# Moving 62 transfers of a transformer kernel from SyncE's queue to GpSimd's

## The chip, the cores and the metric

The kernel runs on one core of a Trainium2 chip, as one program. The metric is device time in microseconds, from several executions: the median of three runs before the change is 4835.77 us (4834.83 to 4836.31). The engines are named as in the profile: PE (TensorE's matmuls; PEld its weight loads), DVE (VectorE), ACT (ScalarE), POOL (GpSimd) and SP (SyncE). SP computes nothing here. It issues transfers between the chip's main memory (DRAM) and the on-chip buffers; POOL and ACT can issue transfers too. An instruction that has to wait holds up all that stands behind it on the same engine.

## The reference

Two layers of a hybrid transformer block over 512 latent tokens and 256 context tokens of width 1024. Cut to what matters:

```python
for l in range(2):
    with_ctx = l < 1                            # layer 1 leaves out the context's branch results
    h_lat = rmsnorm(x_lat, norm1_g[l]) * (1 + sc1) + sh1          # the same for the context
    p = h_lat @ w_in[l]                         # ssm input, q, k, v of two attentions, three gates
    ys, yd, yn = ssm_mixer(...), diff_mixer(...), na_mixer(...)   # three branches
    m = sigmoid(g_ssm) * (ys @ w_br_ssm) + sigmoid(g_diff) * (yd @ w_br_diff) + sigmoid(g_na) * (yn @ w_br_na)
    x_lat = x_lat + g1 * (m @ w_out[l])
    h2 = rmsnorm(x_lat, norm2_g[l]) * (1 + sc2) + sh2
    x_lat = x_lat + g2 * peer_ffn(h2, ...)      # 8 heads x 16 of 16384 experts per token
    # in layer 0 the context tokens go the same way
return rmsnorm(x_lat, final_norm_g)
```

`peer_ffn` scores keys, takes the best 16 pairs for each head, and sums `gelu(u_i . h2) * g_i * v_i` over the chosen experts. All arithmetic is float32.

## The kernel before

Tokens are in six tiles of 128 (0 and 1 context, 2 to 5 latent). The state x, the branches' results, gates, q, k and v are kept in DRAM tensors between the stages: `xs` (one 512 KB entry for each tile), `ybuf` (branch results, eight chunks of 128 channels), `hn` (the next layer's normalised tiles) and others.

**A layer's stages.** `front` makes the normalised tokens `hh`, `hl`, projects, runs the state-space and attention branches, and then merges: `merge` loads the branch results (`yt`, eight loads, two buffers, each split at once into a high part `yh` and a rest `yl`), multiplies by `w_br`, gates, multiplies by `w_out`, adds to x, and stores each tile to `xs`. Layer 0 merges twice (context, latent), layer 1 once; beside layer 0's merges stand the matmuls of the next layer's modulation (`ada_w`). The expert stage follows. `prepared` and `normed` load pairs of tiles from `xs` into the one buffer `nx` of their pool, `root` squares them on ACT and takes the reciprocal root on DVE, `normed_tile` scales (`ny`), transposes on PE and modulates, and the result is split into `h2`. Two pools of this kind are at work in layer 0, one for the latent tiles and one for the context's. Then `early` multiplies all 128 blocks of `peer_u` by `h2` (PE tile `s`), beside the choice of experts (`chosen`, `route`), while tokens of a few tiles (0 and 1 in layer 0, 2 in layer 1) get their experts by gathers (`gathered`, tile `grow`, on POOL). `experts` multiplies 128 blocks of `peer_v` (PE tile `stay`); `finish` adds x to each tile's result and stores it to `xs` in layer 0 (to the output in layer 1); `renew` normalises the tile for layer 1 and stores it to `hn`, from which `front` of layer 1 loads it again.

**Precision.** Each float32 operand is split into two parts (`split`: a cast on ACT, L61, and a subtraction on DVE, L62), and three matmuls are done (L70 to L72). Weights are streamed: `chunk` loads 512 KB into a rotating buffer (`raw`; `row()` takes buffers of the same kind for rows of x) and splits it.

**Queues and order.** All plain transfers, except results of `early` and the gate tables (which ACT issues), go through one helper on SP, so in the profile they all have the line L58:

```python
    def dma(self, out, in_):
        self.nc.sync.dma_start(out, in_)
```

POOL issues only the gathers (L1206). The loops of a stage are woven by hand with costs (`weave`), and that gives each instruction its priority; the final order on each engine is written out when the program is built, by a scheduler that follows priorities and its own model of times. On the chip each engine then runs its list strictly in order, and waits where an operand or a buffer isn't ready. Buffers of a new stage lie where buffers of an old one lay, and wait for those to be read.

Of the kernel before, what the change touches and what calls it, by code (L numbers as in the profile page):

```python
# [50 lines left out]
class Net:  # L51
# [4 lines left out]

    def dma(self, out, in_):
        self.nc.sync.dma_start(out, in_)  # L58

    def split(self, x, hi, lo):  # L60
        self.nc.scalar.copy(hi, x)  # L61
        self.nc.vector.tensor_sub(lo, x, hi.bitcast(F32))  # L62
# [412 lines left out]
    def normed(self, src, r, scale, shift, p, pg):  # L475

        tmp = pg.tile([128, 8, 256], F32, name="ntmp", tag="gst")
        for i, ap in enumerate(src):
            x = p.tile([128, D], F32, name="nx", bufs=1)
            self.dma(x, ap)  # L480
            y = p.tile([128, D], F32, name="ny", bufs=1)
            self.normed_tile(x, y, tmp[:, :, 128 * i:128 * i + 128], r, scale, shift, p)
        return tmp
# [448 lines left out]
    def merge(self, l, x, t0, n, p):  # L932

        nc, v = self.nc, self.nc.vector
        ts = slice(t0, t0 + n)
        yh, yl, mh, ml = [p.tile([128, 8, n], F32R, name=a, bufs=1) for a in ("yh", "yl", "mh", "ml")]
        for k in range(8):
            t = p.tile([128, n], F32, name="yt")
            self.dma(t, self.ybuf[l][k, :, ts])
            self.split(t, yh[:, k], yl[:, k])  # L940
            yield 0.50
        for j in range(4):
            w = self.wchunk(self.a["w_br"][l, j])
            for h in range(2):
                c = slice(128 * h, 128 * h + 128)
                g = p.tile([128, 3, n], F32, name="g3")
                self.dma(g, self.gbuf[l][2 * j + h, :, :, ts])
                for b, (k0, nk) in enumerate(((0, 2), (2, 4), (6, 2))):
                    ps = self.ps1("mg")
                    self.mm3(ps[:, :n], lambda k: (w[0][:, k0 + k, c], w[1][:, k0 + k, c]),  # L950
                             lambda k: (yh[:, k0 + k], yl[:, k0 + k]), nk)
                    v.scalar_tensor_tensor(g[:, b], g[:, b], 1.0, ps[:, :n], op0=ALU.add, op1=ALU.mult)
                    if b:
                        v.tensor_add(g[:, 0], g[:, 0], g[:, b])
                self.split(g[:, 0], mh[:, 2 * j + h], ml[:, 2 * j + h])
            yield 5.00
        tiles = range(t0 // 128, (t0 + n) // 128)
        gate = {}
        for r in sorted({1 if i < 2 else 0 for i in tiles}):
            gate[r] = p.tile([128, D], F32, name=f"g1{r}", bufs=1)  # L960
            self.dma(gate[r], self.arow[l][r:r + 1, 2 * D:3 * D].to_broadcast([128, D]))
        xt = {}
        for i in tiles:
            xt[i] = p.tile([128, D], F32, name=f"x{i - tiles[0]}", bufs=1)
            self.dma(xt[i], x[i])
        for j in range(4):
            w = self.wchunk(self.a["w_out"][l, j])
            c = slice(256 * j, 256 * j + 256)
            for i in reversed(tiles):
                t = slice(128 * i - t0, 128 * i - t0 + 128)  # L970
                ps = self.ps1("mg")
                self.mm3(ps[:, :256], lambda k: (mh[:, k, t], ml[:, k, t]), lambda k: (w[0][:, k], w[1][:, k]), 8)
                d = p.tile([128, 256], F32, name="d")
                v.scalar_tensor_tensor(d, ps[:, :256], 0.5, gate[1 if i < 2 else 0][:, c], op0=ALU.mult, op1=ALU.mult)
                v.tensor_add(xt[i][:, c], xt[i][:, c], d)
            yield 4.00
        for i in reversed(tiles):
            self.dma(self.xs[i], xt[i])

    def part(self, t0, n, x):  # L980
        t = slice(t0, t0 + n)
# [320 lines left out]
    def finish(self, l, i, acc, to):  # L1302

        v, p = self.nc.vector, self.sp
        r = 0 if i > 1 else 1
        if r not in self.gate:
            self.gate[r] = self.row()
            self.dma(self.gate[r], self.arow[l][r:r + 1, 5 * D:6 * D].to_broadcast([128, D]))
        x = self.row()
        self.dma(x, self.xs[i])  # L1310
        v.tensor_mul(to, acc, self.gate[r])  # L1311
        v.tensor_add(to, to, x)  # L1312
        if l < DEPTH - 1:
            self.dma(self.xs[i], to)
        else:
            if "f" not in self.gate:
                self.gate["f"] = self.row()
                self.dma(self.gate["f"], self.a["final_g"].to_broadcast([128, D]))
            v.tensor_scalar_mul(x, to, self.root(to, x, p))  # L1319
            v.tensor_mul(x, x, self.gate["f"])  # L1320
            self.dma(self.out[i - 2], x)

    def renew(self, l, i, x):

        h = self.row().rearrange("p (k t) -> p k t", k=8)
        self.normed_tile(x, self.row(), h, 0 if i > 1 else 1, self.nscale[l + 1][0], self.acol[l + 1][:, 0:8], self.sp, wide=True)
        self.dma(self.hn[i], h)

    def hidden(self, ph):
        self.hh = ph.tile([128, 8, NT], F32R, name="hh")  # L1330
# [2 lines left out]
    def front(self, l):  # L1333

        x = self.a["x"] if l == 0 else self.xs
        kinds = range(l, 2)
        with ExitStack() as right, ExitStack() as left:
            self.hidden(right.enter_context(self.pool("h", side="right")))
            own = right.enter_context(ExitStack())
            if l == 0:  # L1340
                prep = self.ssm_prep(l, own.enter_context(self.pool("sprep", side="right")))
                with self.psum(mm=3, un=3, sm=2), self.pool("norm", 2) as p:
                    self.drain(self.weave((self.start(l, p), 40.0), (prep, 40.0), lead=True))
            else:
                prep = iter(())
                with self.pool("norm", 2, "right") as p:
                    for i in range(6):
                        t = p.tile([128, 8, 128], F32, name="hn")
                        self.dma(t, self.hn[i])
                        self.part(128 * i, 128, t)  # L1350

            def states():
                yield from prep
                own.close()
                with self.pool("ssm", 1, "right") as p:
                    yield from self.ssm(l, p)
                if l < DEPTH - 1:
                    with self.pool("sprep", 1, "right") as p:
                        yield from self.ssm_prep(l + 1, p)

            def mixers(p):
                def attends(u):
                    for g in kinds:
                        yield from self.attend(l, g, u, p)

                cost = 84.0 if l == 0 else 72.0
                yield from self.project(l, 0, p)
                yield from self.weave((self.project(l, 1, p), 48.0), (attends(0), cost))
                yield from self.weave((self.project(l, 2, p), 48.0), (attends(1), cost))
                yield from attends(2)  # L1370

            pg = left.enter_context(self.pool("gate"))
            with self.stream(3, 4), self.psum(sc=2, mm=3, sm=2, gt=1), self.pool("att") as p:
                self.att_consts(l, p)
                self.drain(self.weave((mixers(p), 500.0 if l == 0 else 450.0), (states(), 300.0 if l == 0 else 200.0),
                                      (self.gates(l, pg), 187.0 if l == 0 else 125.0)))
        with self.stream(3, 4), self.psum(mg=5, mm=3), self.pool("next", 2) as q:
            def merges():
                for g in kinds:
                    with self.pool("mg", 2) as p:  # L1380
                        yield from self.merge(l, x, LCTX * g, LLAT if g else LCTX, p)

            jobs = [(merges(), 70.0)]
            if l < DEPTH - 1:
                jobs.append((self.modulation(l + 1, range(24), q), 72.0))
            self.drain(self.weave(*jobs))
# [174 lines left out]
```

## Time and profile before

| what | value |
|---|---|
| median of three runs | 4835.77 us |
| profiled execution | 4839.11 us, its span 4837.2 us |
| mean granted TensorE clock | 0.956 |
| PE busy | 4437.8 us (92%) |
| DVE busy | 3786.0 us (78%) |
| ACT busy | 1849.3 us (38%) |
| POOL busy | 1130.1 us (23%) |
| bytes moved | 1215.18 MB, mean 251 GB/s |

The shares are of the whole span; a stage can have quite another limit. The page shows PE at 70 to 80% in a few of its 40 slices, at the passages between stages, and POOL at nothing outside the gathers' two stretches. SP's instructions are all issues of transfers: the time beside one is that of the issue, not of the transfer. A merged row (x4) spans from the first of its instructions to the end of the last.

### The profile page before, as it was taken

Reading aid. Unit: us, or ns where it says so; the run is one execution under the profiler, and the core shown is the slowest. Engines: PE = TensorE matmul, PEld = TensorE weight load, DVE = VectorE, ACT = ScalarE, POOL = GpSimd, SP = SyncE. Lnnn points to the kernel's source line nnn. Section 1 sums busy time; section 2 is a strip of 40 time slices with the busy share of each in tenths; the row PEclk is TensorE's granted clock in tenths of the full one; section 3 lists DMA queues with packets and bytes.
Section 4 is the critical chain, followed back from the end, with each engine's and each line's share of the span. In section 5 each row is a group of like instructions: output and inputs, shape, how many; then the busy total and the mean of one; then the engine's idle time right before and its main releaser. Section 6 shows DMA issues by size and latency. Waiting matters only on the chain. (4 is left out here: it accounts for less than half of the span.)

```text
span 4837.2 us, 68859 instructions
## 1 busy us (share of the span) xinstructions
PE 4437.8 (92%) x24197; PEld 3718.5 (77%) x24197; DVE 3786.0 (78%) x8760; ACT 1849.3 (38%) x3019; POOL 1130.1 (23%) x772
## 2 busy tenths in 40 slices
PE   8998998869988999879999998999879999989998
PEld 4787886668776777658888877887769899978887
DVE  8377985758988999987887764877555799968888
ACT  3244454434322345443222223445233355533333
POOL 0000000000465355533343300000000133324552
PEclk9999998979999999989999998999889999999999
DMA  7453435844898789999999945533444599989997
GB/s 244 153 146 99 144 118 178 271 149 134 301 334 306 253 317 335 360 351 377 361 339 351 344 173 176 147 118 97 169 133 144 174 338 351 344 325 379 371 374 269
DMA packets 462839, 1215.18 MB, mean 251 GB/s; under 512 B 47691, under 2 KB 181915, under 8 KB 458907
## 3 DMA queue, kind: packets, MB, share of 16 engines
q1 hardware_dynamic: 311002, 690.61, 41.9%
q0 software_dynamic: 110592, 402.70, 22.7%
q10 hardware_dynamic: 40896, 117.46, 6.2%
q8 instruction: 190, 3.11, 0.3%
q14 instruction: 159, 1.29, 0.1%
HBM read 1031.54 MB, written 179.04 MB: 250 GB/s over the span
## 5 line engine op out<-in xcount | busy, mean ns | idle before, releaser
L1206 POOL DMA_INDIRECT grow<-in_u_rows,pick x384 | 515.3, 1342 | 2944.3 <-DVE cand L1078 1201.7
L61 ACT CAST hi<-raw 128x1024 fp32r<-128x1024 f32 x490 | 513.2, 1051 | 893.0 <-PE s L71 590.5
L62 DVE TENSOR_TENSOR lo<-raw,hi 128x1024 fp32r<-128x1024 f32 x490 | 595.5, 1218 | 290.5 <-ACT hi L61 287.2
L72 PE MATMUL s<-h2h,lo 128*128 128x512 f32 (+1 forms) x2048 | 762.4, 373 | 54.6 <-DVE lo L62 54.2
L70 PE MATMUL s<-h2h,hi 128*128 128x512 f32 (+1 forms) x2048 | 772.2, 377 | 12.3 <-ACT eact L1244 9.2
L1206 POOL DMA_INDIRECT grow<-in_v_rows,pick x384 | 614.7, 1601 | 696.6 <-PE stay L1277 251.0
L71 PE MATMUL s<-h2l,hi 128*128 128x512 f32 (+1 forms) x2048 | 761.4, 372 | 0.2 <-DVE h2l L62 0.2
L1274 PE MATMUL stay<-hiv,wh 128*128 128x512 f32 x1792 | 709.1, 396 | 48.4 <-ACT hiv L61 48.4
L1275 PE MATMUL stay<-lov,wh 128*128 128x512 f32 x1792 | 709.0, 396 | 0.0
L1228 DVE SCALAR_TENSOR_TENSOR row<-grow,gw,row 128x1024 f32<-128x1024 f32 x381 | 487.7, 1280 | 100.1 <-DMA grow<-in_v_rows,pick 98.8
L1277 PE MATMUL stay<-hiv,wl 128*128 128x512 f32 x1792 | 563.2, 395 | 0.3 <-DVE wl L62 0.3
L1220 DVE SCALAR_TENSOR_TENSOR grow<-grow,row 128x1024 f32<-128x1024 f32 x384 | 462.6, 1218 | 98.5 <-DMA grow<-in_u_rows,pick 98.0
L72 PEld LDWEIGHTS s<-h2h,lo 128*128 128x128 f32 x2048 | 391.5, 191 | 112.1 <-DVE lo L62 66.7
L61 ACT CAST wh<-w 128x512 fp32r<-128x512 f32 (+1 forms) x256 | 145.2, 567 | 775.5 <-DVE w L1264 396.2
L70 PEld LDWEIGHTS s<-h2h,hi 128*128 128x128 f32 x2048 | 392.1, 191 | 60.1 <-ACT eact L1244 14.5
L1274 PEld LDWEIGHTS stay<-hiv,wh 128*128 128x128 f32 x1792 | 338.7, 189 | 127.4 <-ACT hiv L61 48.7
L71 PEld LDWEIGHTS s<-h2l,hi 128*128 128x128 f32 x2048 | 391.6, 191 | 44.1 <-DVE h2l L62 0.6
L1275 PEld LDWEIGHTS stay<-lov,wh 128*128 128x128 f32 x1792 | 338.7, 189 | 80.3 <-DVE lov L62 1.3
L1277 PEld LDWEIGHTS stay<-hiv,wl 128*128 128x128 f32 x1792 | 338.3, 189 | 79.8 <-DVE wl L62 0.9
L62 DVE TENSOR_TENSOR lov<-raw,hiv 128x1024 fp32r<-128x1024 f32 x256 | 312.0, 1219 | 6.3 <-ACT hiv L61 6.3
L61 ACT CAST hiv<-raw 128x1024 fp32r<-128x1024 f32 x256 | 267.9, 1047 | 67.5 <-DMA raw<-in_peer_v 67.3
L1264 DVE TENSOR_TENSOR w<-act,gt 128x512 f32<-128x512 f32 (+1 forms) x256 | 158.6, 620 | 108.1 <-DMA act<-actd 106.5
(430 smaller groups left out, 8733.8 us busy)
## 6 DMA issues: line engine op xcount, KB each, us to landing
raw<-in_peer_u SPq DMA_DIRECT2D x256, 512.0 KB
raw<-in_peer_v SPq DMA_DIRECT2D x256, 512.0 KB
gd<-gst ACTq DMA_DIRECT2D x28, 2048.0 KB
raw<-in_w_in SPq DMA_DIRECT2D x88, 512.0 KB
actd<-eact ACTq DMA_DIRECT2D x128, 256.0 KB
gt<-gd SPq DMA_DIRECT2D x16, 2048.0 KB
act<-actd SPq DMA_DIRECT2D x128, 256.0 KB
adaw<-in_ada_w SPq DMA_DIRECT2D x48, 512.0 KB
```

What stands on the lines that cost most here:

```text
L61: self.nc.scalar.copy(hi, x)
L62: self.nc.vector.tensor_sub(lo, x, hi.bitcast(F32))
L70: mm(ps, lh, rh, start=start and k == 0, stop=False)
L71: mm(ps, lh, rl, start=False, stop=False)
L72: mm(ps, ll, rh, start=False, stop=stop and k == n - 1)
L1206: d = nc.gpsimd.indirect_dma_start(out=t, out_offset=None, in_=self.a[table], in_offset=bass.IndirectOffsetOnAxis(ap=picks[y][0][:, j:j + ...
L1220: v.scalar_tensor_tensor(t, t, 1.0, h, op0=ALU.mult, op1=ALU.mult, accum_out=u[:, j:j + 1])
L1228: v.scalar_tensor_tensor(h, t, w[:, j:j + 1], h, op0=ALU.mult, op1=ALU.add)
L1264: v.tensor_mul(w.rearrange("p (b t) -> p b t", t=32), act.rearrange("p (b t) -> p b t", t=32), self.gt[:, :, i % 8])
L1274: nc.tensor.matmul(ps[:, c], wh[:, t], vh[:, c], start=i == 0, stop=False)
L1275: nc.tensor.matmul(ps[:, c], wh[:, t], vl[:, c], start=False, stop=False)
L1277: m = nc.tensor.matmul(ps[:, c], wl[:, t], vh[:, c], start=False, stop=i == 127)
```

## The change

A second helper issues on GpSimd, and seven calls use it: the nx loads, the yt loads, the xs stores of `merge` and `finish`, the hn stores of `renew`, and the hn loads of `front`. In all 62 transfers: 10 nx loads, 24 yt loads, 10 + 6 xs stores, 6 hn stores, 6 hn loads. All others stay where they were. What depends on what is unchanged.

```diff
@@ -56,6 +56,10 @@
     def dma(self, out, in_):
         self.nc.sync.dma_start(out, in_)
+
+    def pass_on(self, out, in_):
+
+        self.nc.gpsimd.dma_start(out, in_)
@@ normed
             x = p.tile([128, D], F32, name="nx", bufs=1)
-            self.dma(x, ap)
+            self.pass_on(x, ap)
@@ merge
             t = p.tile([128, n], F32, name="yt")
-            self.dma(t, self.ybuf[l][k, :, ts])
+            self.pass_on(t, self.ybuf[l][k, :, ts])
...
         for i in reversed(tiles):
-            self.dma(self.xs[i], xt[i])
+            self.pass_on(self.xs[i], xt[i])
@@ finish
         if l < DEPTH - 1:
-            self.dma(self.xs[i], to)
+            self.pass_on(self.xs[i], to)
@@ renew
-        self.dma(self.hn[i], h)
+        self.pass_on(self.hn[i], h)
@@ front
                         t = p.tile([128, 8, 128], F32, name="hn")
-                        self.dma(t, self.hn[i])
+                        self.pass_on(t, self.hn[i])
```

## Rows read from the trace of the kernel before

**Rows 1.** The page, part 1: busy us, share of span, instructions
```profile
PE 4437.8 (92%) x24197; PEld 3718.5 (77%) x24197; DVE 3786.0 (78%) x8760; ACT 1849.3 (38%) x3019; POOL 1130.1 (23%) x772
```

**Rows 2.** Windows: length, PE, PEld, DVE, ACT, POOL busy, clock, DMA share, GB/s
```profile
1037.00:1082.00 45.00, 10.26 (x42) 8.28 (x42) 26.82 (x95) 20.80 (x34) 0.00 (x0) 0.58 0.57 193
...
2870.00:2930.00 60.00, 29.05 (x135) 23.30 (x134) 35.75 (x101) 23.72 (x42) 0.00 (x0) 0.70 0.49 170
...
3388.00:3420.00 32.00, 17.01 (x41) 10.71 (x42) 12.98 (x18) 9.15 (x14) 0.00 (x0) 0.55 0.79 264
...
3504.00:3550.00 46.00, 9.96 (x41) 8.42 (x42) 23.02 (x70) 19.90 (x32) 0.00 (x0) 0.52 0.48 166
```

**Rows 3.** SP's waits over the span: us in total, times, longest
```profile
SPq L58 <- DVE x L975: 64.6, 12, 25.6
...
SPq L58 <- DVE ny L487: 40.4, 7, 11.2
```

**Rows 4.** Timeline of SP, 1040 to 1067: start us, us, instruction
```profile
1040.16 0.80 SPq L58 DMA_DIRECT2D nx<-xs  x2
...
1048.16 0.33 SPq L58 DMA_DIRECT2D nx<-xs  x1
...
1058.21 0.33 SPq L58 DMA_DIRECT2D nx<-xs  x1
...
1066.15 0.33 SPq L58 DMA_DIRECT2D nx<-xs  x1
```

**Rows 5.** Timelines of ACT, then SP (idle before and its releaser in brackets)
```profile
1044.02 1.06 ACT L506 ACTIVATE ny<-nx 128x1024 f32<-128x1024 f32 x1 [30.56 <-DMA nx<-xs]
...
3530.71 1.09 ACT L506 ACTIVATE ny<-nx 128x1024 f32<-128x1024 f32 x1
...
3524.48 11.87 SPq L58 DMA_DIRECT2D nx<-xs  x2
```

**Rows 6.** Timeline of POOL; then tile `grow`, window 1201:1203, and whole span
```profile
1203.45 0.94 POOL L1206 DMA_INDIRECT grow<-in_u_rows,pick  x1 [0.30 <-issue]
...
1235.74 1.99 POOL L1206 DMA_INDIRECT grow<-in_u_rows,pick  x1 [0.30 <-issue]
...
DMA to landing us min/median/max: 6.6/6.6/6.6
...
DMA to landing us min/median/max: 4.4/7.7/17.6
```

**Rows 7.** Timelines of SP, ACT and PE, merge of layer 1
```profile
3389.53 0.88 SPq L58 DMA_DIRECT2D yt<-ybuf  x2
...
3396.91 0.93 SPq L58 DMA_DIRECT2D yt<-ybuf  x2
...
3388.23 1.99 ACT L61 CAST hi<-raw 128x1024 fp32r<-128x1024 f32 x2
...
3400.58 0.62 ACT L61 CAST yh<-yt 128x512 fp32r<-128x512 f32 x1 [4.52 <-DMA yt<-ybuf]
...
3395.59 0.79 PE L70 MATMUL mg<-yh,hi 128*128 128x512 f32 x1 [7.67 <-ACT yh L61]
```

**Rows 8.** Timelines of PE and ACT, merges of layer 0
```profile
911.57 0.79 PE L70 MATMUL mg<-yh,hi 128*128 128x512 f32 x1 [2.48 <-ACT yh L61]
...
775.91 0.94 ACT L61 CAST yh<-yt 128x256 fp32r<-128x256 f32 x2 [2.87 <-DMA yt<-ybuf]
...
789.61 0.58 PE L70 MATMUL mg<-yh,hi 128*128 128x256 f32 x1
```

**Rows 9.** Timelines of SP and PE, end of layer 0
```profile
2883.71 6.28 SPq L58 DMA_DIRECT2D hn<-raw  x2
2890.08 0.38 SPq L58 DMA_DIRECT2D raw<-xs  x1
...
2921.37 0.38 SPq L58 DMA_DIRECT2D raw<-in_w_in  x1
...
2928.41 0.79 PE L70 MATMUL mm<-hi,hh 128*128 128x256 f32 x2 [15.17 <-ACT hi L61]
```

## The prediction

> **What bounds the kernel now.** Read first the page's busy shares: PE is busy for 4437.8 us of 4837.2 [rows 1], so only the roughly 400 us in which PE stands still can be won, and whatever lengthens them is paid in full. Then the stretches around the moved transfers [rows 2]: at both handovers from a merge to the expert stage PE works 10 of 45 us, at the end of layer 0 29 of 60, in layer 1's merge 17 of 32. POOL's column is 0.00 in all four, so its queue is empty when the moved transfers arrive, and none but moved transfers stand behind one that waits: the gathers come in other stretches, and in layer 0 all of them are issued before `finish` stores. Last, SP's own waits [rows 3]: 64.6 us for the sums that an xs store needs and 40.4 us for `ny`, which frees the buffer of the next nx load. Such waits are what the change takes off SP. The question is whether PE was short of something held up behind them, or of the waiting transfer itself.
>
> **What PE waits for at the handovers.** The first nx loads are issued at 1040.16, and the load of each further tile of the same pool at 1048.16, 1058.21 and 1066.15 [rows 4], when `ny` has read the one nx buffer (that at 1054.73, between them, belongs to the other pool). So this is a loop: load, square on ACT, reciprocal root on DVE, `ny`, next load; its last pass took 7.94 us. The load is 3.86 us of it, from 1040.16 to ACT's start at 1044.02 [rows 4, 5]. The chain is made of moved transfers: the store, four loads, and what hangs on them. What is freed on SP beside it, the expert weights, PE can't use before the normalised tokens are there.
>
> **The cost of one transfer on GpSimd's queue, called d: what it takes more than on SP.** No plain GpSimd transfer is in the trace; the nearest rows are gathers of the same 512 KB [rows 6]. The first one, into an idle queue, landed after 6.6 us, the quickest of all after 4.4 us. Against 3.86 that makes d 0.54 to 2.74 us. A gain is excluded: POOL works 0.94 us on a gather at the least, and SP was done with an nx load in 0.33. I take d = 1.5, between the ends and a little nearer the low one, since a plain transfer reads no list of indices.
>
> The Trainium skill, page "DMA: Bandwidth & Descriptors", section "Latency and other measured facts", has a first byte after about 0.6 us on the hardware path and about 1 us on GpSimd's, 0.4 us apart (an estimate from these two figures); by it the sum below would be next to nothing. The landing of the lone gather speaks for more. The case is the first rival below.
>
> **The sum, place by place.**
>
> 1. Handover in layer 0: one store and four loads in series, 5 d = 7.5 us. Back: the pass from 1048.16 to 1058.21 took 10.05 us against 7.94 [rows 4], with weight splits between its steps that could now run before it; I count half of the 2.1 us, 1.0. Net +6.5.
> 2. Handover in layer 1: the same chain, but the third load, issued at 3524.48, is read by ACT only at 3530.71, 6.2 us later, not for lack of data but after another operation [rows 5], so its d is covered. 4 d = 6.0, less 1.0 of the same kind: +5.0. Without that cover 1.5 more.
> 3. Merge of layer 1: eight yt loads in four pairs, two buffers. The second pair goes out at 3396.91 and is cast at 3400.58 [rows 7]; PE waits for each pair, so the three later rounds cost 3 d = 4.5. The first pair, at 3389.53, stood on SP behind the last attention store and can now start earlier. PE waited 7.67 us for it, until 3395.59; if yh were cast straight after the two weight casts that end at 3390.2, PE would start at about 3391.0, 4.6 earlier. Another weight cast may stay ahead of it on ACT, so I count half, 2.3. Net +2.2.
> 4. Second merge of layer 0: PE waits for yh as well, 2.48 us [rows 8]; two rounds count, 2 d = +3.0.
> 5. First merge of layer 0: nothing. The last yh casts start at 775.91, PE's first matmul on them at 789.61 [rows 8]; the 12.8 us between the casts' end and it hide four rounds of d, and fail to for d over 3.
> 6. End of layer 0: an x load at 2890.08 stood on SP behind two `hn` stores that held it for 6.0 us, and the next layer's first weight load at 2921.37, while PE had been idle since 2913.24 (2928.41 less 15.17), waiting for its cast in the end [rows 9]. At best both waits go, -6.0 and -8.1. At worst three steps through `hn` grow by d, +4.5: its stores and reloads stay in one queue and in their order. The buffers' reuse decides, which no row shows; I take -1.0, near nothing.
> 7. The xs stores of `finish`: nothing, nobody reads xs until layer 1's merge, hundreds of us later.
>
> Sum: 6.5 + 5.0 + 2.2 + 3.0 - 1.0 = 15.7, or 14 d less 5.3. The profiled execution took 4839.11 us, its span and 1.9 around it; 15.7 more is 4854.8. The median of three runs is 3.3 lower, 4835.77, and it is that which is forecast: 4851 us. The ends of d give 14 x 0.54 - 5.3 = +2.3, 4838, and 14 x 2.74 - 5.3 = +33.1, 4869.
>
> One more thing moves the result: the order in which each engine's instructions stand is written out by a scheduler when the program is built, which models times; with other queues neighbours may swap places on ACT and DVE. The covered third load of place 2 shows what such an order is worth: some 2 us each. A few of them, either way, are inside the range.
>
> **The rivals.**
>
> *The extra latency is small* (d = 0.54): +2.3, 4838 us, no change to be told. For it: the quickest gather. Against it: the lone gather's 6.6 us. The same time results if the change does little at all, the waits merely standing in another queue.
>
> *Faster: late prefetch is what PE waits for.* Place: the end of layer 0 and layer 1's merge. The x loads and the next layer's weights come as soon as SP could have issued them (-6.0 and -8.1), yh is cast before the last weight chunk (-4.6), and 2.0 comes from the two handovers: 20.7 us. With d = 0.54 in 14 places, 7.6, that leaves -13.1: 4823 us. It decides where d is under 20.7 / 14 = 1.48 us, if all of it comes. For it: the gaps of 15.17 and 7.67 us are real, and what ended them had been held on SP. Against it: the new stage's weight buffers may lie where the last tiles' rows still lie.
>
> *VectorE delays GpSimd.* Beside VectorE's two-input work POOL took 1.99 us for a gather instead of 0.94 [rows 6], 1.05 more, and splits and sums stand beside most moved transfers. Then d is at its upper end: +33.1, 4869 us. Against it: an nx load is issued when VectorE has just finished `ny`.
>
> The Trainium skill ("SBUF — State Buffer", section "SBUF: two separate sides") says that descriptors of a transfer issued from GpSimd can't be written while VectorE holds the port pair that both share. The slow gather agrees in direction, though it also reads indices; by the rule at its worst the time is the 4869 of this rival.
>
> **How the numbers follow.** Forecast 0.48 (own range 4843 to 4869, d from 0.9 up), small latency 0.22, faster 0.19, VectorE's delay 0.11. A measurement of this kernel tells about 0.2%, 9.7 us, from no change: 4826 to 4845. Slower by more holds the third rival and the forecast but for 0.05 of it: 0.54. Within it 0.22 + 0.05 = 0.27. Faster 0.19. For eight in ten I go down to 4820, which leaves out the outer part of the faster case, and up to 4875, a little past the upper end of d.
>
> **What would show it.** Right: a plain 512 KB transfer issued on POOL is read over 5 us after its issue; nx loads stand about 9.5 us apart; the gap from the last merge matmul to the first on h2 grows by about 6 us in layer 0 and 5 in layer 1; SP has no wait for xs sums and `ny`, and issues expert weights before 1037 without PE's resuming sooner. Wrong: nx loads still 8 us apart (d is small); the gaps that end at 2928 and 3395 shrinking by more than 5 us each (the prefetch was the bound); or the expert stages, from 1082 and from 3550 on, changing their length by more than 5 us, of which nothing here is forecast.

## The result, and the profile after

The changed kernel takes 4864.25 us (median of five runs, 4856.2 to 4867.64) against 4836.31 us (the kernel before, median of five runs taken with them): the ratio is 1.0052, with a 95% interval from 1.0041 to 1.0064, or 20 to 31 us lost. The forecast was 4851 us, slower, in a range from 4820 to 4875. The profiled execution after has a span of 4864.0 us, 26.8 more than before.

The work is the same, only POOL has 62 instructions more; PE's busy time moved by 1.6 us [rows 1].

```profile
PE 4436.2 (91%) x24197; PEld 3709.8 (76%) x24197; DVE 3787.2 (78%) x8760; ACT 1847.2 (38%) x3019; POOL 1146.5 (24%) x834
```

So PE stood still for longer. The stretches of [rows 2] after, the handovers from the last merge matmul to some 42 matmuls on, as there:

```profile
1039.50:1091.50 52.00, 9.55 (x41) 8.01 (x41) 25.87 (x93) 19.62 (x33) 3.71 (x7) 0.57 0.46 154
2879.50:2940.00 60.50, 28.65 (x133) 22.84 (x132) 35.41 (x100) 23.51 (x42) 9.24 (x16) 0.71 0.52 186
...
3519.50:3577.00 57.50, 9.77 (x42) 8.23 (x42) 23.79 (x72) 18.52 (x31) 2.65 (x5) 0.52 0.40 129
```

and the 32 us from the start of layer 1's merge:

```profile
3398.50:3430.50 32.00, 13.42 (x28) 8.04 (x28) 10.81 (x14) 8.05 (x12) 4.29 (x8) 0.51 0.71 264
```

PE does its ten microseconds of work at the handovers in 52 and 57.5 us, where 45 and 46 held it before, and 13.42 us of work in the merge's 32, where it did 17.01. Both kernels start 24197 matmuls, in the same order outside the merges and the first 30 us of layer 1. The start of the k-th of them after, less its start before, is the delay at that point; its growth over a stage is what the stage lost. Worked out so from PE's instructions:

```
us, after against before               measured   forecast
up to the first merge                    -0.1        0
layer 0, first merge                     +1.2        0
layer 0, second merge                    +1.5       +3.0
layer 0, handover to the experts         +7.6       +6.5
layer 0, peer_u stage                    -3.9        0
layer 0, peer_v stage                    +3.0        0
end of layer 0                           +1.4       -1.0
layer 1, front                           -0.5        0
layer 1, merge                           +6.1       +2.2
layer 1, handover to the experts        +12.3       +5.0
layer 1, peer_u and peer_v stages        -1.4        0
```

The last row but one counts 10.7 us up to the first matmul on the normalised tokens and 1.6 in the products right behind it. The wait ahead of the first normalised tile at layer 1's handover, before and after:

```profile
3515.51 1.97 PE L492 MATMUL mm<-ident,ny 128*128 128x128 f32 x8 [12.46 <-DVE ny L487]
```

```profile
3540.46 1.76 PE L496 MATMUL mm<-ident,ny 128*128 128x128 f32 x7 [20.96 <-DVE ny L491]
```

**Where it is lost.** At layer 0's handover, POOL's timeline against [rows 4]; columns are start, us, instruction, and in brackets the idle time before it and what ended it:

```profile
1037.60 0.53 POOL L62 DMA_DIRECT2D xs<-x  x1 [2.34 <-DVE x L979]
1040.47 0.53 POOL L62 DMA_DIRECT2D xs<-x  x1 [2.34 <-DVE x L979]
1049.01 1.14 POOL L62 DMA_DIRECT2D nx<-xs  x2 [8.00 <-DMA xs<-x]
1058.41 0.53 POOL L62 DMA_DIRECT2D nx<-xs  x1 [8.27 <-DVE nrst L523]
...
1067.50 0.53 POOL L62 DMA_DIRECT2D nx<-xs  x1 [1.32 <-DVE ny L491]
1076.75 0.53 POOL L62 DMA_DIRECT2D nx<-xs  x1 [8.72 <-DVE ny L491]
```

The last store of x is issued at 1040.47, and the first load of nx, which has to wait for it to land, at 1049.01, 8.5 us later. Before it was 2.6 us (the last of four stores at 1037.53, the load at 1040.16 [rows 4]). The landing itself, 0.5 us ahead of the load's issue, came 8.0 us after the store's. The load itself is no slower: issued at 1049.01, read by ACT at 1052.83,

```profile
1052.83 1.06 ACT L510 ACTIVATE ny<-nx 128x1024 f32<-128x1024 f32 x1 [25.45 <-DMA nx<-xs]
```

3.82 us later, against 3.86 before. Only the time from `ny` to the next issue is longer, 0.5 us instead of 0.06. So one transfer of the chain lost more than five microseconds, and the others half of one on average: from the first of these loads to the last in the list it is 27.7 us, where it was 26.0. What moved beside the store stands on SP:

```profile
1037.86 0.33 SPq L58 DMA_DIRECT2D raw<-in_peer_wq  x1
1038.29 0.38 SPq L58 DMA_DIRECT2D raw<-in_peer_u  x1
1038.71 20.73 SPq L58 DMA_DIRECT2D raw<-in_peer_wq  x3
```

Before, these weight loads stood behind the first nx load, which waited for the store (SP before, the four stores in one row; between the rows stands the nx load of 1040.16):

```profile
1028.90 8.95 SPq L58 DMA_DIRECT2D xs<-x  x4
...
1041.05 0.38 SPq L58 DMA_DIRECT2D raw<-in_peer_u  x1
1041.53 0.92 SPq L58 DMA_DIRECT2D raw<-in_peer_wq  x2
```

Now SP waits neither for sums nor for `ny` there and issues the first three of them ahead of the last store. At layer 1's handover the DMA engines show what that does. Two views by queue, first of the 4.7 us after the store's issue at 3520.72, then of the 3.4 us up to its landing (q1 is SP's queue, q0 POOL's):

```profile
q1 hardware_dynamic: 321, 1.20, 91.9%
```

```profile
q1 hardware_dynamic: 241, 0.88, 63.6%
q0 software_dynamic: 144, 0.52, 37.7%
```

For 4.7 us not one packet of the store moves, while SP's queue carries 1.20 MB of expert weights; then both share the engines. Those weights are for PE, which can't use them before the tokens that the store delays.

**Layer 1's merge** shows the same on the yt loads (POOL's issues, then ACT's casts; compare [rows 7]):

```profile
3408.47 1.14 POOL L62 DMA_DIRECT2D yt<-ybuf  x2 [8.75 <-DVE yl L66]
3416.15 0.54 POOL L62 DMA_DIRECT2D yt<-ybuf  x1 [6.54 <-DVE yl L66]
...
3423.25 1.22 POOL L62 DMA_DIRECT2D yt<-ybuf  x2 [5.25 <-DVE yl L66]
```

```profile
3414.51 0.62 ACT L65 CAST yh<-yt 128x512 fp32r<-128x512 f32 x1 [7.15 <-DMA yt<-ybuf]
...
3421.61 1.23 ACT L65 CAST yh<-yt 128x512 fp32r<-128x512 f32 x2 [5.17 <-DMA yt<-ybuf]
3426.26 1.24 ACT L65 CAST yh<-yt 128x512 fp32r<-128x512 f32 x2 [3.42 <-DMA yt<-ybuf]
```

The second pair is cast 6.0 us after its issue and the third 5.5, against 3.7 and 3.6 before; the fourth, 13 us after SP's last load was issued, after 3.0, against 5.3 before, when it stood on SP with the loads of x right behind it.

### The profile page after: what moved, and what is told of

Read it like the earlier page. It is cut to its first block, busy times and chain, and to the rows that moved or that the text cites. A ratio compares the mean times of both kernels' runs of the same rounds, so it can differ in the third digit from the quotient of the medians.

```text
span 4864.0 us, 68926 instructions
## 1 busy us (share of the span) xinstructions
PE 4436.2 (91%) x24197; PEld 3709.8 (76%) x24197; DVE 3787.2 (78%) x8760; ACT 1847.2 (38%) x3019; POOL 1146.5 (24%) x834
## 5 line engine op out<-in xcount | busy, mean ns | idle before, releaser
L1210 POOL DMA_INDIRECT grow<-in_v_rows,pick x384 | 598.6, 1559 | 709.7 <-PE stay L1281 259.8
L62 POOL DMA_DIRECT2D yt<-ybuf x24 | 13.1, 547 | 1276.7 <-DVE vl L66 718.9
```

The source lines that it names most:

```text
L62: self.nc.gpsimd.dma_start(out, in_)
L1210: d = nc.gpsimd.indirect_dma_start(out=t, out_offset=None, in_=self.a[table], in_offset=bass.IndirectOffsetOnAxis(ap=picks[y][0][:, j:j + ...
```

## The experiments

Theory A: what costs is that SP, freed of the waits, issues loads of weights that then move ahead of and beside the moved transfers. Theory B: GpSimd's queue is slow by itself. All experiments are the changed kernel with some of its seven calls set back to `self.dma`, unless more is said; each was compared with the kernel before on the same chip, whose own runs there went from 4824 to 4853 us. "Handover" is the time from the last merge matmul to the first on the normalised tokens: 44.45 us in layer 0 and 46.52 in layer 1 before, 52.21 and 57.25 in the changed kernel, so 7.8 and 10.7 us more. (The 12.3 us in e1's expectation have the 1.6 us behind that matmul in them.)

```
                       ratio  (95% interval)     handover L0   handover L1
e1  stores, nx         1.0033 (1.0020, 1.0047)     51.19         56.75
e2  stores             0.9989 (0.9978, 1.0000)     45.48         46.98
e3  nx                 1.0028 (1.0016, 1.0040)     51.67         56.13
e4  stores, nx on ACT  1.0031 (1.0017, 1.0044)     49.87         56.66
e5  yt                 1.0008 (0.9999, 1.0017)     44.48         46.53
e6  tail               0.9999 (0.9990, 1.0007)     46.68         46.52
e7  e1, first nx on SP 1.0015 (1.0005, 1.0026)     52.04         50.97
e8  all but nx         1.0019 (1.0010, 1.0027)     44.55         47.03
e9  e1 and weights     1.0009 (1.0000, 1.0018)     48.05         48.90
e10 as e2              0.9990 (0.9980, 1.0000)     44.79         47.44
e11 stores, tail       1.0012 (1.0003, 1.0021)     45.15         47.22
e12 two first stores   1.0003 (0.9994, 1.0012)     44.32         46.60
```

**e1, the handovers alone.** The merges' stores of x and the nx loads on POOL.

```diff
-            self.pass_on(t, self.ybuf[l][k, :, ts])
+            self.dma(t, self.ybuf[l][k, :, ts])
...
-            self.pass_on(self.xs[i], to)
+            self.dma(self.xs[i], to)
```

(`hn` likewise.)

> Only the stores of x in the merges and the nx loads go through GpSimd's queue; branch results, finish and hn stay on SyncE's. Both theories expect the two handovers to be as in the changed kernel: the gap from the last merge matmul to the first on the normalised tokens 7.8 us longer in layer 0 and 12.3 us longer in layer 1, less the 3.9 us that layer 0's expert stage gave back there: +16, 4852 us. If the merges' or the tail's part of the change belongs to these sums too, it is under 4845.

Measured 4855.68 us against 4837.92, 16 us by the ratio, as expected. Most of the loss is here. The last stores land 7.9 us (layer 0) and 8.3 us (layer 1) after their issue.

**e2, the stores without the nx loads.**

```diff
-            self.pass_on(x, ap)
+            self.dma(x, ap)
```

(against e1)

> Only the stores of x in the merges go through GpSimd's queue; the nx loads stand on SyncE's again, with the expert weights behind them. Theory A (the store is late because the weight loads that SyncE is now free to issue are moved beside it): the weights wait behind the first nx load again, so the last store lands some 3 us after its sum, not 8.3; both handovers grow by at most 1 us each, total 4836 to 4839 us. Theory B (a store through GpSimd's queue takes 8 us by itself): it lands after 8 us, both gaps grow by 5.5 us, total 4844 to 4848 us.

Measured 4834.6 us, 1.4 us below A's range: theory B falls. Each last store lands 2.9 us after its issue, on the same queue as in e1. SP's timeline in layer 0 says why: the nx loads stand ahead of the weights again.

```profile
DMA to landing us min/median/max: 2.9/2.9/2.9
```

```profile
1037.54 0.80 SPq L58 DMA_DIRECT2D nx<-xs  x2
1038.45 0.37 SPq L58 DMA_DIRECT2D raw<-in_peer_u  x1
1038.91 0.95 SPq L58 DMA_DIRECT2D raw<-in_peer_wq  x2
```

**e3, the nx loads without the stores.** The other half of e1.

```diff
-            self.pass_on(self.xs[i], xt[i])
+            self.dma(self.xs[i], xt[i])
```

> Only the nx loads go through GpSimd's queue; the stores of x stand on SyncE's, ahead of the expert weights. Theory A (collision with the released weights): the last store lands in 2.6 us as before, but the weight loads issued right behind it are under way when the first nx load is issued, so that load takes 5.5 to 8 us instead of 3.9; with 0.5 us for each of the further loads each handover grows by 3 to 6 us, total 4841 to 4846 us. Theory B (GpSimd's own latency): every load, the first too, costs the 0.5 us more that the changed kernel's later loads showed; +2 us for each handover, total 4838 to 4841 us.

Measured 4851.06 us, 13.5 us by the ratio: A in kind, but more than A put on it, since the handovers grew by 7.2 and 9.6 us instead of 3 to 6. The delay is now on the load, which lands 7.9 us after its issue in layer 0, with five weight loads issued on SP ahead of it.

```profile
1035.40 0.32 SPq L58 DMA_DIRECT2D xs<-x  x1
1035.82 0.37 SPq L58 DMA_DIRECT2D raw<-in_peer_u  x1
1036.29 1.24 SPq L58 DMA_DIRECT2D raw<-in_peer_wq  x2
1037.58 0.42 SPq L58 DMA_DIRECT2D raw<-in_peer_u  x1
1038.05 5.12 SPq L58 DMA_DIRECT2D raw<-in_peer_wq  x2
```

```profile
1038.98 1.27 POOL L62 DMA_DIRECT2D nx<-xs  x2 [1038.52 <-DMA xs<-x]
```

```profile
1046.86 1.06 ACT L510 ACTIVATE ny<-nx 128x1024 f32<-128x1024 f32 x1 [5.31 <-DMA nx<-xs]
```

In the 4 us after that load's issue, SP's queue moved 1.37 MB and POOL's one packet. In layer 1 the second load too was late, landing 6.6 us after its issue, which neither theory had counted.

**e4, the same transfers on ScalarE's queue**, which is a hardware queue like SP's.

```diff
-        self.nc.gpsimd.dma_start(out, in_)
+        self.nc.scalar.dma_start(out, in_)
```

(against e1)

> The same transfers as in the first of these kernels (stores of x in the merges, nx loads), but through ScalarE's queue, a hardware queue as SyncE's is. Theory A (collision with released weights): SyncE is as free as with GpSimd, the last store still lands 6 to 8 us after its issue; the handovers grow by nearly as much, total 4846 to 4851 us. Theory B (GpSimd's own latency): the store lands in 2.6 us and loads take 3.9, nothing is lost at the handovers, total 4835 to 4838 us.

Measured 4849.74 us, as A expected. GpSimd isn't needed for the loss: on ACT's queue the last store of layer 1 is issued at 3501.83 and lands when the load goes out, 7.7 us later.

```profile
3501.83 0.33 ACTq L62 DMA_DIRECT2D xs<-x  x1
3509.51 0.33 ACTq L62 DMA_DIRECT2D nx<-xs  x1
```

**e9, the released weights put behind again, all on GpSimd's queue.** As e1, and the first weight loads of the expert stage go through POOL too. The order written out for POOL there is SP's of before: stores, nx, weights, nx, weights.

```diff
-            w = self.wchunk(self.a["peer_wq"][l, h])
+            w = self.wchunk(self.a["peer_wq"][l, h], self.pass_on if h < 4 else None)
...
-                  self.chunk(self.a["peer_u"][l, i].rearrange("p k j -> p (k j)"))]
+                  self.chunk(self.a["peer_u"][l, i].rearrange("p k j -> p (k j)"), on=self.pass_on if i < 8 else None)]
```

> As e1_handover (stores of x in the merges and nx loads through GpSimd's queue), and the expert stage's first weight loads (the first four heads' peer_wq and the first eight blocks of peer_u) go through GpSimd's queue too, so that they stand behind the nx loads again as they did on SyncE's. Theory A (collision of two queues): the last store lands after 2.9 us, each nx load is read 4.4 us after what frees its buffer, 0.5 more than on SyncE's; layer 0's handover grows by 2 us (0.3 for the store, four loads by 0.5) and layer 1's by 2; beyond the handovers, between 1100 and 2170, peer_wq behind gathers may cost something that says nothing of this. Total 4838 to 4843 us. Theory B (GpSimd's queue is slow by itself): the store takes 8 us as in e1_handover, both handovers grow by 6 us or more, 4852 us or above.

Measured 4839.83 us, ratio 1.0009. This is the deciding run: e1's transfers stay on GpSimd's queue, and three quarters of e1's loss is gone. Layer 1's stretch on POOL:

```profile
3503.90 0.53 POOL L62 DMA_DIRECT2D xs<-x  x1 [2.34 <-DVE x L979]
3507.52 0.54 POOL L62 DMA_DIRECT2D nx<-xs  x1 [3.08 <-DMA xs<-x]
3508.30 1.07 POOL L62 DMA_DIRECT2D raw<-in_peer_wq  x2 [0.24 <-issue]
3509.37 1.60 POOL L62 DMA_DIRECT2D raw<-in_peer_u  x3
3517.12 0.54 POOL L62 DMA_DIRECT2D nx<-xs  x1 [6.16 <-DVE ny L491]
```

The store is waited for 3.1 us instead of 8.4. The handovers still are 3.6 and 2.4 us longer than before, where 2 and 2 were expected. GpSimd's own price is in this, and not alone: layer 0's last store landed after 3.5 us there, and layer 0's handover is 2.2 us longer in e6 too, which doesn't touch it.

**e7, holding the weights with one load.** As e1, but the first nx load of each pair is back on SP.

```diff
-            self.pass_on(x, ap)
+            (self.pass_on if i else self.dma)(x, ap)
```

> Stores of x in the merges and nx loads through GpSimd's queue, as in e1_handover, but the first nx load of each pair of tiles is back on SyncE's queue, ahead of the expert weights. Theory A: with the weights held behind that load the last store lands after 3 us again, and both handovers are within 3 us of the kernel before; what is left is 0.5 to 1 us for each of the second loads: 4835 to 4842 us. Theory C (the extra queue itself, with its issue and its semaphores, is what costs): no better than e1_handover but for the one load, 4850 to 4856 us.

Measured 4843.71 us, between e1 and the kernel before. That is 1.7 us above A's range, and the expectation of 3 us for each handover failed, with 7.6 and 4.5. The stores land in 2.9 us as A says, but the weights then go out behind the first load, and the second, on POOL, meets them:

```profile
1043.83 0.54 POOL L62 DMA_DIRECT2D nx<-xs  x1 [10.76 <-ACT hi L65]
```

```profile
DMA to landing us min/median/max: 7.2/7.2/7.2
```

The hold moved the collision by one transfer.

**e8, all but the nx loads**, the change with one call set back.

> The change but for the nx loads, which stay on SyncE's queue ahead of the expert weights. Theory A: nothing is lost at the handovers (store of x landing after 3 us), what is left is the merges' yt loads and the tail: 4838 to 4844 us. Theory B (each transfer costs on GpSimd's queue): the stores, yt and hn keep their part, 4850 to 4856 us.

Measured 4845.64 us, nearer to A's numbers and 2 us above them. One call of the seven carries 0.33% of 0.52%, and both handovers are about as long as before. Layer 1's merge loses 6.1 us as in the changed kernel. Its yt loads to their landing, first those issued from 3402 to 3416, under SP's weight, gate and x loads, then those from 3418 to 3424, when SP had issued the last of these 13 us before:

```profile
DMA to landing us min/median/max: 5.1/5.8/6.6
```

```profile
DMA to landing us min/median/max: 2.8/2.9/2.9
```

One queue, one kind of transfer, half the time when the other queue is done.

**e5, only yt.**

> Only the loads of branch results (yt) go through GpSimd's queue. Theory A (collision with the loads that SyncE is free to issue): a pair of yt under the w_br, gate and x loads takes 6 us to its cast instead of 3.7, and layer 1's merge grows by 5 to 6 us, layer 0's two merges by 1 to 3 together: total 4842 to 4846 us. Theory B (GpSimd's own latency of 0.5 us a transfer): three rounds in layer 1 and two in layer 0 cost 2.5 us in all: 4838 to 4840 us.

Measured 4840.09 us, ratio 1.0008: the time doesn't decide. The trace has layer 1's merge 7.0 us longer, with a pair of yt landing 8.1 and 8.8 us after its issue, and other stretches shorter by 14 us together, layer 0's peer_u stage, which no edit touches, by 8.2 alone.

**e6, only the end of layer 0** (`finish`, `renew`, `hn`).

> Only the end of layer 0 is changed: the stores of finish, and the stores and loads of hn go through GpSimd's queue. The changed kernel lost 1.4 us between the last product with peer_v and layer 1's projections, and both theories expect that here: 4836 to 4839 us. Rival (late prefetch is what PE waits for there): the gap at layer 1's first weights closes by up to 14 us, 4822 us.

Measured 4834.42 us, ratio 0.9999: nothing, where both theories had 1.4 us, which is too little to tell; the gain by prefetch isn't there.

**e10, e11, e12, what may be left to win.** e10 is e2 once more, e11 adds the tail to it, and e12 moves only the stores of layer 0's first merge:

```diff
-            self.dma(self.xs[i], xt[i])
+            (self.pass_on if l == 0 and t0 == 0 else self.dma)(self.xs[i], xt[i])
```

> e2_store_only once more, for its size: there the ratio to the kernel before was 0.9989, between 0.9978 and 1.0000. If SyncE, freed of the two stores of layer 0's first merge, gains what the trace of e2_store_only showed in the second merge (some 3 us), the ratio is 0.9990 to 0.9996 again; if that was chance, 1.0000.

> The stores of x in the merges and the end of layer 0 (finish, hn) through GpSimd's queue; yt and nx loads on SyncE's. The two parts measured alone were 0.9989 and 0.9999: 0.9988, 4830 us, if they add up and are real; 1.000 if the first was chance.

> Only the two stores of x of layer 0's first merge go through GpSimd's queue; both handovers are as in the kernel before. If the gain in layer 0's second merge (some 3 us) comes from SyncE no longer standing at these stores, ratio 0.9990 to 0.9996; if not, 1.0000.

e10 gave 0.9990 again, e11 1.0012 and e12 1.0003. The stores alone may be worth 5 us, but both intervals reach 1.0000. What the trace of e2 suggested as the cause, the two stores of the first merge, gives nothing by itself. The tail cost nothing alone, and yet e11, the stores with the tail, came out above both values expected; why wasn't found. No version is shown to beat the kernel before.

## Why the prediction was right, and what of it was wrong

The direction, the range and the places held: most of the loss is at the handovers and in layer 1's merge, and the expert stages changed by less than 5 us each. The size was short, 15.7 us forecast against 26.8, and the cause behind it was another.

**d, 1.5 us for every transfer: wrong in kind.** There is no one price. With nothing else on its way, a store on POOL is issued 0.28 us after its sum and lands 2.9 us after that (e2, and layer 1 in e9), 3.2 in all against 2.6 on SP. An nx load is issued 0.5 us after its release and read 3.8 us later, 4.3 against 3.9. So d is about 0.5 us, the low end that I had from the quickest gather. Beside loads of SP's queue it went from 1.2 us (e1's second nx load of layer 1, landing after 5.0 us instead of 3.8) to 5.9 (a yt load of e5, landing after 8.8 instead of 2.9); the last stores lost 5.4. The sum of fourteen equal terms came within a factor of 1.7 because a few transfers at the large price and the rest at the small one make a like amount, which is luck. On an idle queue the first packet of a store moved 1.1 us after its issue on POOL (3517.84 to 3518.96) and 0.8 us on SP (1034.66 to 1035.48 before). The Trainium skill, "DMA: Bandwidth & Descriptors", "Latency and other measured facts", has the first bytes of the two paths 0.4 us apart (an estimate from its two figures), and the trace, with 0.3, nearly agrees.

**The step that failed** is the clause "what is freed on SP beside it, the expert weights, PE can't use before the normalised tokens are there". I booked the released loads as no gain, and left out that they use the same DMA engines. e3 and e4 show the loss without the store on GpSimd and without GpSimd; e2 shows it gone, and e9 three quarters of it, as soon as the weights stand behind the nx load. Place by place:

1. Layer 0's handover, +6.5 forecast, +7.6 measured. The one store took 5.4 us more, and the loads half a microsecond each on average, not 1.5. The credit of 1.0 came, as PE's second gap shrank from 8.08 to 7.12 us, but 1.0 was lost ahead of it: between the steps of the first tile's root DVE now has a step for the other pool's tile, and stood still for 0.95 us, until 1056.09, for that tile's square. Nearly right by accident.
2. Layer 1's, +5.0 forecast, +12.3 measured, 10.7 of it up to the first matmul on the normalised tokens. The gap ahead of the first transposed tile alone grew from 12.46 to 20.96 us, by 8.5; 5.4 of that is the store, and 2.0 came from DVE, where the order written out now has three weight splits between the steps of the root, not one. So the weights that came earlier took the credit of 1.0 back instead of giving it. The second load, beside three weight loads on SP, took 5.9 us from issue to ACT, against 4.8 before. The cover of the third load was there: it is read at 3557.18, 5.8 us after its issue, when ACT has ended a cast, and PE's gap is as long as before. The last 1.6 us are the first products: from 3580.4 to 3583.8 they ran at a granted clock of 0.51 (1.2 GHz), and the same ones before, from 3553.3 to 3555.2, at 1.00 (2.4 GHz), in both kernels after a handover in which PE mostly stood still. The twelve other kernels lose 0.1 to 1.4 us there, so this part need not be the change's.
3. Layer 1's merge, +2.2 forecast, +6.1 measured. The credit of 2.3 didn't come: the first pair of yt goes out 0.1 us after the last attention matmul, which it has to wait for, and the weight cast that I had as a chance is still ahead of it on ACT. PE waited 8.32 us there instead of 7.67. Two of the later rounds cost 2.6 and 2.2 us instead of 1.5, by the collision, and the last gave 1.9 back. Another 2.7 us were lost further on, while PE took up the products with w_out. Matmuls at a granted clock of 0.51 (1.2 GHz) from 3478.0 to 3481.4, which before ran at 1.00 (2.4 GHz), are 1.4 of it; the rest wasn't followed. The kernels that leave yt on SP lose from -0.8 to +3.9 us there, so these 2.7 can't be put down to the moved loads.
4. The merges of layer 0, 0 and +3.0 forecast, +1.2 and +1.5 measured. In the experiments the two together went from -8.9 to +6.2 us, and by -2.4 and -2.3 in e3 and e6, which change nothing there, so little can be said at this size.
5. End of layer 0, -1.0 forecast, +1.4 measured. In e6 the time didn't change, but its trace has this stretch 4.4 us longer, and the kernels that don't touch it lie between -1.1 and +3.2, so neither sign is shown. The first weight chunk was issued at 2916.76, which is 22 us ahead of where PE first uses it and 14 us earlier, less the delay so far, than at 2921.37 [rows 9]. PE waited 16.01 us for its cast all the same, against 15.17:

```profile
2934.32 1.04 ACT L65 CAST hh<-hn 128x1024 fp32r<-128x1024 f32 x1 [5.51 <-DMA hn<-hn]
2935.39 1.28 ACT L672 ACT_TABLE_LOAD   x1
...
2936.79 1.03 ACT L65 CAST hh<-hn 128x1024 fp32r<-128x1024 f32 x1
2937.72 1.99 ACT L65 CAST hi<-raw 128x1024 fp32r<-128x1024 f32 x2
```

The cast of the chunk stands behind four casts of `hh`, which wait for hn, and the order on ACT, not the load, sets the time.

**The signs.** The nx loads of layer 0 stood 9.1 to 9.4 us apart, near the 9.5 forecast, yet not by the mechanism forecast: on the chain they were read 3.8 to 4.7 us after their issue, where the forecast had over 5. The handovers grew by 7.8 and 10.7 us up to the first matmul on h2, where it had 6 and 5. None of the signs of being wrong came.

**The rivals.** "Small latency" had the right d, and its 4838 us is near what e9 takes, where SP's weights don't collide. "Late prefetch" had its condition met (d under 1.48) and its transfers came earlier as it said, at the end of layer 0 and at both handovers, yet PE gained nothing: e6, and item 5. "VectorE delays GpSimd" isn't seen in the one case at hand: in e8 a pair of yt was issued at 3419.04, while VectorE was in a two-input subtraction until 3419.38, and the first of it landed in 2.8 us.

**What stays open.** Layer 0's peer_v stage lost 3.0 us with PE never idle and the granted clock at 1.00: 687 or 688 matmuls in each 160 us, against 690 or 691 before.

```profile
2346.50:2506.50 160.00, 160.00 (x688) 128.69 (x687) 129.08 (x150) 44.19 (x58) 58.12 (x47) 1.00 0.96 347
```

The same stage is 2 to 4 us longer in e1, e2, e10 and e11 and within 0.7 us of before in the eight others, with no edit that these four share alone; the cause wasn't found. Layer 0's peer_u stage was 0.3 to 8.2 us shorter than before in every kernel profiled, e6 among them, which doesn't touch what leads to it. So the -3.9 there is rather the one profile of before than the change.

## What to carry to other kernels

A transfer that waits in an in-order queue also holds back what stands behind it, and that can be worth keeping: before a latency-bound transfer gets a queue of its own, list what the old queue will issue the moment it is free, and ask whether that will move on the same DMA engines ahead of it. Put the urgent transfer and the bulk loads behind it on one queue, in that order, whichever engine issues them. And price a move from the landing times of the same kind of transfer with and without neighbours, not by one average latency.

## What the runs showed that was not expected

Two queues did not share the DMA engines from the moment of the second one's issue. A 512 KB store issued on POOL while SP's loads were on their way moved no packet for 4.7 us, while 1.20 MB of the other queue passed, and then took 3.4 us at about a third of the engines. On ACT's queue it was alike in e4: in the 4.3 us after 3501.9 SP's queue moved 0.98 MB and ACT's 0.02. The Trainium skill ("DMA: Bandwidth & Descriptors", "Queues, rings and completion order") has each DMA engine take turns between the queues that have work for it, packet by packet; the rows agree for the second stretch and not for the first, and the cause of the first wasn't tried. When the store's first packet moved, 1.3 of the 1.57 MB that SP had issued ahead of it had gone.

A plain transfer takes POOL 0.53 us to issue and SP 0.33. A lone 512 KB store on POOL landed 2.9 us after its issue (e2), against the 6.6 us of the lone gather from which I had bounded d above.
